# Query tiles in pairs, value products over 512 queries, and one written order for five engines in a hybrid attention block

## The chip, the cores and the metric

The kernel runs on one core of a Trainium2 chip. The metric is the time of one execution on the device, in microseconds; the time of a version is the median of its runs. A profiled execution gives a span, from the first to the last instruction, and a record of each instruction on TensorE (PE, with PEld for its weight loads), VectorE (DVE), ScalarE (ACT), GpSimd (POOL) and SyncE (SP, which issues DMAs).

## The reference

One block of a model with 512 tokens of 1024 features, all in float32. Two attention branches work on one projection of the normalised input and are merged by gates; an output projection and a feed-forward part with squared relu follow, each added to the residual.

```python
n = rmsnorm(h, g_mix[l])
proj = n @ w_in[l]
(gq, gk, gv, gr, z_gf, z_gb, cq, ckv, kr, z_ma, z_mb) = jnp.split(proj, SPLIT_IDX, axis=-1)
y_gla = gla_branch(...)
y_mla = mla_branch(cq, ckv, kr, positions, g_q[l], w_uq[l], g_kv[l], w_ukv[l])
merged = jax.nn.sigmoid(z_ma) * y_gla + jax.nn.sigmoid(z_mb) * y_mla
h = h + merged @ w_out[l]
m = rmsnorm(h, g_mlp[l])
h = h + jnp.square(jax.nn.relu(m @ w_ff1[l])) @ w_ff2[l]
...
return rmsnorm(h, g_final)
```

`gla_branch` is linear attention with 4 heads in both directions. `mla_branch` is softmax attention with 8 heads: queries of 96 features (64 and 32 that are rotated by position), keys of the same make, values of 128.

```python
def attend(qblk):
    s = jnp.einsum('bhqd,bhkd->bhqk', qblk, kt).astype(jnp.float32)
    p = jax.nn.softmax(s, axis=-1)
    return jnp.einsum('bhqk,bhkv->bhqv', p.astype(vt.dtype), vt)
```

## The kernel before, in words

**Numbers in two parts.** Almost every product is made of three matmuls in the type fp32r (`mm3`, L87 to L90): each operand is split into a high part (a copy in fp32r, on ACT) and a remainder (a subtraction, on DVE or POOL; `split`, L92 to L94), and high times high, high times remainder and remainder times high are added up in PSUM. So each line L88, L89 or L90 in the profile is one of the three, and L93 and L94 are the two halves of a split. Tiles ending in h and l, or pairs of tiles, are these parts.

**Stages.** First come the input projections, with a seven-product scheme for large blocks (`Seven`). Then a loop over the first three linear heads, and the fourth, last one behind it (L1310 on), among which the latent projections for the softmax heads, the rotary tables and the gates zb4 to zb7 are made. From L1350 the softmax attention runs, with the first products of the output projection at its end; then the rest of the output projection (`wo_product`, seven products m over two row blocks, in the PSUM tiles wox, wow and woz) and its row statistics (hp). From L1888 the feed-forward part runs, eight phases f0, g0 to f3, g3, whose steps are written with due times and sorted. `last_rows` ends it: the last product of the last phase, and the final rmsnorm.

**Softmax attention.** A head is in `heads` with its query tile q (one tile of two parts, 128 x 2 x 512, made in `up_units` from uq and the rotated rows ro, which SP copies into its rows 64 to 95), its keys kbuf, and its values. Four query tiles of 128 each go through these steps, one loop turn n a tile:

- `att_scores` (L1095): three matmuls into s, the row maximum (top, L1102, DVE), the exponential with the row sum (e, L1107, ACT).
- `att_normalise` (L1110), for two tiles: the reciprocal and two scalings, one on ACT (L1113), one on DVE (L1114).
- `att_flip` (L1116), three turns after the scores: four transposes (L1122) of e into tp, split into pT, a pair of tiles for each half of the queries.
- `att_values` (L1127), six turns after: for one half, 256 queries, and four key blocks, 12 matmuls of 256 columns into av.
- `merge` (L1143), once for both halves (for head 7 once for each): the gate times av on DVE (tb, L1150), and two additions on POOL (mx, my, L1153). After every second head `merged_sums` makes yo and zo on POOL, and these and mx are split into gao, ghyo and glyo, ghzo and glzo, the left sides of the output projection.

**What sets the order.** A scheduler orders each engine's instructions unless the code holds it. `in_program_order` ties an engine's instructions from one point on into one chain; `goes_behind` places one group behind another on some engines. PE, ACT and DVE are held to the written order up to the gate zb7 and then again from L1790 on; in between, in attention, PE, ACT and DVE are the scheduler's, apart from a dozen `goes_behind`. POOL is chained in program order from `pooled`, with another chain from `attending`. SP is chained from `stepped` on. `last_rows` has a chain of its own (L1786), which on POOL isn't tied to what stands before it: its first instructions can be placed among the last steps of the feed-forward part.

**The tail.** For each of four row blocks i there are: the sum of squares of the right half (`out_first`, L1713, ACT) and of the left (`out_square`, L1723, ACT); the mean of the first (`out_mean`, L1717, POOL); the row times the gain for the right half (`out_gained`, L1720, POOL); the factor (`out_rstd`: L1727 on DVE, the power L1730 on POOL); the left half (`out_left`, L1734, DVE), the right half (`out_right`, L1738, ACT) and the stores (L1743). The left half of block 3 is made in two parts of 256 columns, gend0 and gend1, each added by L1754; L1776 takes its mean and first part together.

Of the kernel before, what the change touches and what calls it, by code (L numbers as in the profile page):

```python
# [18 lines left out]
P = 128  # L19
# [35 lines left out]

@with_exitstack
def tile_block(ctx: ExitStack, tc: tile.TileContext, t, out: bass.AP):
    nc = tc.nc
# [76 lines left out]
    make_identity(nc, ident)  # L135
# [887 lines left out]
    def up_units(pr):  # L1023

        wq = stage(3, P, f"wq{pr}")
        for k in range(3):
            nc.sync.dma_start(
                wq[:, k, :].rearrange("p (h e) -> p h e", h=2), w_uq[:, k, 2 * pr : 2 * pr + 2, 0:NOPE]
            )
        wqh, wql = halves(3, P, f"wq{pr}")  # L1030
        split(wqh, wql, wq, nc.gpsimd)
        wk = stage(2, 384, f"wk{pr}")
        nc.sync.dma_start(
            wk.rearrange("p k (h e) -> p k h e", h=2), w_ukv[:, :, 2 * pr : 2 * pr + 2, :]
        )
        wh, wl = halves(2, 384, f"wk{pr}")
        src = wk.rearrange("p k (h e) -> p k h e", h=2)
        for k in range(2):
            for c, e in ((slice(0, 128), slice(0, NOPE)), (slice(128, 384), slice(NOPE, 192))):
                split(wh[:, k, c].rearrange("p (h e) -> p h e", h=2),  # L1040
                      wl[:, k, c].rearrange("p (h e) -> p h e", h=2), src[:, k, :, e], nc.gpsimd)
        if pr == 0:
            yield
        def rotary_rows(i):
            h = (2 * pr + i) * HALF
            for x in range(2):
                at = NOPE + x * HALF
                nc.sync.dma_start(raw(qs[i][at : at + HALF]), raw(ro[x][h : h + HALF]))

        apart = pr in (0, MH // 2 - 1)
        qs = [u4(f"q{pr}{i}") for i in range(2)]
        for i in range(2):
            if apart or i == 1:
                rotary_rows(i)
        yield
        accq = up_T(wqh, wql, cq, f"uq{pr}")
        if apart:
            for i in range(2):  # L1060
                split_scaled(qs[i][0:64, 0, :], qs[i][0:64, 1, :], accq[i * 64 : i * 64 + 64, :], QK_SCALE)
        else:
            split_scaled(qs[0][:, 0, :], qs[0][:, 1, :], accq, QK_SCALE)
# [31 lines left out]
    def att_scores(head, qt):  # L1095
        q, kb, _, _ = heads[head]
        tok = slice(qt * P, (qt + 1) * P)
        acc = ps("at", f"s{head}{qt}")
        d = slice(0, NOPE + ROPE)
        mm3(acc, q[d, 0, tok], q[d, 1, tok], kb[d, 0, :], kb[d, 1, :], True, True)  # L1100
        top = sm("top", 1)
        nc.vector.tensor_reduce(top, acc, axis=AX.X, op=ALU.max, negate=True)  # L1102
        e = u2(f"e{head}{qt}")
        if qt % 2 == 0:
            tots[head] = sm("tot", 2)
# [10 lines left out]
    def att_flip(head, qt):  # L1116
        e = probs.pop((head, qt))
        if qt % 2 == 0:
            pTs[head, qt // 2] = [u4(f"pT{head}{qt}{x}", F32R, (P, NT, 256)) for x in range(2)]
        tp = ps("at", f"tp{head}{qt}")  # L1120
        for k in range(NT):
            nc.tensor.transpose(tp[:, k * P : (k + 1) * P], e[:, k * P : (k + 1) * P], ident)  # L1122
        hi, lo = pTs[head, qt // 2]
        c = slice((qt % 2) * P, (qt % 2 + 1) * P)
        split(hi[:, :, c], lo[:, :, c], tp.rearrange("p (k q) -> p k q", k=NT))

    def att_values(head, half):  # L1127
        if half == 0:
            avs[head] = ps("mm", f"av{head}")
        acc = avs[head]  # L1130
        hi, lo = pTs.pop((head, half))
        _, _, vs, c = heads[head]
        for k in range(NT):
# [3 lines left out]
        if head < MH - 1:  # L1137
            if half == 1:
                merge(head, acc, (0, 1))
        else:  # L1140
            merge(head, acc, (half,))
# [167 lines left out]

    h = GH - 1  # L1310
# [27 lines left out]
    first_units = traced()  # L1338
# [3 lines left out]
    first_units = first_units, traced()  # L1342
    at = traced()
    zb = proj_run(w_b, xT)
    last_gate = at, traced()
    g2.append(gated(zb, "b7")[1])
    in_program_order(fixed, SPLITTERS)
    in_program_order(ordered, PE_ONLY)
    in_program_order(pooled, (mybir.EngineType.Pool,))
# [14 lines left out]
    at = traced()  # L1364
    next(units)
    goes_behind((at, traced()), first_units, SPLITTERS[:1])
    attending = traced()
    sums_of, flipping, span = {}, {}, {}
    for n in range(4 * MH + LAG_C - 1):
        if n % 2 == 0 and 2 <= n <= 4 * MH:  # L1370
            att_normalise((n - 2) // 4, (n - 2) % 4)
        scored = traced()
        if n < 4 * MH:
            att_scores(n // 4, n % 4)
            if n - 2 in flipping:
                goes_behind((scored, traced()), flipping[n - 2], SPLITTERS)
        scored = scored, traced()
        if n == 0:
            goes_behind(scored, last_gate, PE_ONLY)
        if n == 3:  # L1380
            span["fourth"] = scored
        if 2 <= n % 8 < 7:
            at = traced()
# [3 lines left out]
            if n < 4:  # L1387
                goes_behind((at, traced()), scored, PE_ONLY)
        if n in (6, 14):
            units = up_units(n // 8 + 2)  # L1390
            at = traced()
            next(units)
            if n == 6:
                goes_behind((at, traced()), span["fourth"], SPLITTERS[:1])
        b = n - LAG_B
        if n == 30:
            xs_ = wo_accs[1] = [ps("mm", f"wox{rb}") for rb in range(2)]
            at = traced()
            wo_product(1, ps_=(0,))
            begun = at, traced()  # L1400
            goes_behind(begun, scored, PE_ONLY)
        if 0 <= b < 4 * MH:
            flips = traced()
            att_flip(b // 4, b % 4)
            flipping[n] = flips, traced()
            if n == 30:
                goes_behind(flipping[n], begun, PE_ONLY)

        if n == 20:
            load_onto(B11, B12, w_out)  # L1410
        extra = traced()
# [8 lines left out]
        if n < 4 * MH:  # L1420
            goes_behind((extra, traced()), scored, SPLITTERS[:1])
# [7 lines left out]
        if n == 17:  # L1429
            at = traced()  # L1430
            load_wo(B21, B22)
            span["sums"] = at, traced()
# [6 lines left out]
        if c >= 0 and c % 2 == 1:  # L1439
            valued = traced()  # L1440
            att_values(c // 4, (c % 4) // 2)
            valued = valued, traced()
        if n == 35:
            at = traced()
            split_first(wo_left[2], merged[2][0], "o2")
            goes_behind((at, traced()), valued, SPLITTERS[1:])
# [298 lines left out]
    def last_rows(ph):  # L1745

        begun = traced()
# [10 lines left out]
        for i in (2, 3):  # L1758
            out_first(i)
        out_gained(2)  # L1760
        out_mean(2)
# [8 lines left out]
        out_mean(3)  # L1770
# [3 lines left out]
        out_store(1)  # L1774
        p = hparts[3]
        nc.vector.scalar_tensor_tensor(p[:, 2:3], p[:, 1:2], 1.0 / D, p[:, 2:3], op0=ALU.mult, op1=ALU.add)  # L1776
        last_part(1)
# [8 lines left out]
        in_program_order(begun)  # L1786

    begun = traced()  # L1790
# [8 lines left out]
    att_values(MH - 1, 1)  # L1799
# [8 lines left out]
    at = traced()  # L1808
    f0.load(B11)
    goes_behind((at, traced()), span["sums"], SP_ONLY)  # L1810
# [74 lines left out]
    for x in range(2):  # L1885
        f0.lo(2, x)
        m_lo(2, x)
    FIRST, SECOND, PERIOD = 36, 22.77, 7857  # L1888
# [75 lines left out]
    stepped = traced()  # L1964
# [34 lines left out]
```

## Time and profile before

| | us |
|---|---|
| runs | 738.37, 738.38, 739.01 |
| median | 738.38 |
| profiled execution | 739.02 |
| its span | 737.3 |
| first written instruction of the changed stretch on PE (products bd) | 254.6 |
| last matmul starts | 728.32 |

A line of a timeline gives start, duration, engine, line, operation, the tiles written and read, the shapes, and in square brackets how long the engine sat idle before it and whose work ended that. A line of the groups gives the count, the busy time, the mean duration in ns, then the idle time before them. A line of a table by stretches gives the stretch, its length, busy time of PE, PEld, DVE, ACT and POOL, each with the number of instructions, the clock that was granted to PE, the busy share of the DMA engines and GB/s. A wait gives who waited, for whom, the sum in us, how often, and the longest.

### The profile page before, as it was taken

To read this page: it belongs to the slowest core of one execution; us is meant where nothing else is said; L and a number is where in the kernel's file an instruction comes from. 1 tells how busy PE (TensorE), PEld (TensorE's weight loads), DVE (VectorE), ACT (ScalarE), POOL (GpSimd) and SP (SyncE) were. 2 spreads that over 40 slices of the span, in tenths; PEclk is the share of its full clock that TensorE was granted. 3 is DMA by queue.
4 is the path that set the end of the run, shared out by engine and by line. 5 is a ranking of instruction groups with operands and counts; after the bars stand their busy time and mean duration, and the time that the engine had idled before them with its cause. 6 is when DMAs were issued, how large, how long until landed. Compare 5 with 4: busy or idle time off the path is not lost.

```text
span 737.3 us, 11473 instructions
## 1 busy us (share of the span) xinstructions
PE 726.9 (99%) x4226; PEld 643.1 (87%) x4226; DVE 625.0 (85%) x861; ACT 494.2 (67%) x809; POOL 220.7 (30%) x284
## 2 busy tenths in 40 slices
PE   9999999999999999999999999999999999999995
PEld 7888888888888888899888899889988998899984
DVE  7777787889988788798898889998699869987896
ACT  7557465595696675988856879545874477537764
POOL 0732020243743724126852511200211012101215
PEclk9999999999999999999999999999999999999999
DMA  9849682431222324557978899862987088815773
GB/s 309 277 100 215 215 188 90 79 64 31 58 58 58 51 72 89 127 111 214 291 145 233 133 267 185 184 204 63 250 181 192 20 240 175 196 57 146 170 114 114
DMA packets 80520, 109.95 MB, mean 149 GB/s; under 512 B 15920, under 2 KB 34352, under 8 KB 80464
## 3 DMA queue, kind: packets, MB, share of 16 engines
q1 hardware_dynamic: 63088, 75.64, 32.9%
q0 software_dynamic: 17088, 33.30, 27.1%
q8 instruction: 33, 0.54, 0.3%
q10 hardware_dynamic: 288, 0.28, 0.1%
q14 instruction: 23, 0.19, 0.1%
HBM read 104.22 MB, written 2.10 MB: 144 GB/s over the span
## 4 chain that ended last, share of the span: by engine, by line
PE 88%; DVE 5%; issue 2%; POOL 2%; ACT 1%; DMA 1%; POOLq 0%; DVEq 0%; ACTq 0%
PE first L326 3%; PE tp L1122 2%; PE zb L88 1%; PE zb L89 1%; PE zb L90 1%; PE f2x L90 1%; PE f3x L90 1%; PE f1x L90 1%; PE f3x L89 1%; PE f2x L89 1%; PE f1x L89 1%; PE f1x L88 1%; PE f3x L88 1%; PE f2x L88 1%; PE av L89 1%
## 5 line engine op out<-in xcount | busy, mean ns | idle before, releaser
L1626 POOL DMA_DIRECT2D w<-in_w_ff x40 | 48.3, 1240 | 254.9 <-DMA w<-in_w_ff 139.3
L1102 DVE TENSOR_REDUCE top<-s 128x1 f32<-128x512 f32 x32 | 21.6, 682 | 4.9 <-PE s L90 4.7
L1107 ACT ACTIVATE e<-s,top 128x512 f32<-128x512 f32 x32 | 21.9, 687 | 3.5 <-DVE top L1102 2.6
L94 DVE TENSOR_TENSOR pT<-tp,pT 128x512 fp32r<-128x512 f32 x32 | 21.8, 682 | 2.4 <-ACT pT L93 2.0
L93 ACT ACTIVATE pT<-tp 128x512 fp32r<-128x512 f32 x32 | 19.0, 595 | 3.2 <-PE tp L1122 3.2
L1122 PE MATMUL tp<-ident,e 128*128 128x128 f32 x128 | 19.4, 274 | 0.0
L88 PE MATMUL av<-pT,v 128*128 128x256 f32 x64 | 19.1, 299 | 0.0
L90 PE MATMUL av<-pT,v 128*128 128x256 f32 x64 | 18.2, 285 | 0.0
L89 PE MATMUL av<-pT,v 128*128 128x256 f32 x64 | 18.1, 284 | 0.0
L1122 PEld LDWEIGHTS tp<-ident,e 128*128 128x128 f32 x128 | 15.2, 140 | 3.1 <-ACT e L1113 0.7
L94 POOL TENSOR_TENSOR qF<-qk,qF 128x512 fp32r<-128x512 f32 x4 | 6.6, 1641 | 37.6 <-ACT qF L93 37.6
L667 POOL DMA_DIRECT2D gvw<-in_w_in x4 | 4.8, 1230 | 38.7 <-DVE gvw L672 34.0
L667 POOL DMA_DIRECT2D zaw<-in_w_in x4 | 4.9, 1228 | 32.7 <-DVE zaw L672 28.0
L1628 DVE TENSOR_TENSOR w<-w,w 128x1024 f32<-128x1024 f32 x12 | 14.4, 1220 | 0.1
L980 POOL DMA_DIRECT2D w<-in_w_out x10 | 12.2, 1400 | 6.5 <-DVE bo60l L94 5.3
L88 PE MATMUL s<-kbuf,q 96*128 96x512 f32 x32 | 14.1, 439 | 0.0
L1153 POOL TENSOR_TENSOR mx<-tb,yg 128x256 f32<-128x256 f32 x8 | 7.7, 964 | 19.8 <-DVE tb L1150 13.9
L577 ACT ACTIVATE bds<-bd 128x512 f32<-128x512 f32 x4 | 2.4, 597 | 15.8 <-PE bd L555 15.8
L89 PE MATMUL s<-kbuf,q 96*128 96x512 f32 x32 | 12.6, 395 | 0.0
L90 PE MATMUL s<-kbuf,q 96*128 96x512 f32 x32 | 12.6, 393 | 0.0
L1113 ACT ACTIVATE e<-e,tot 128x512 f32<-128x512 f32 x16 | 11.6, 726 | 1.3 <-DVE tot L1112 1.3
L89 PEld LDWEIGHTS av<-pT,v 128*128 128x128 f32 x64 | 12.2, 191 | 0.2
(2156 smaller groups left out, 3250.4 us busy)
## 6 DMA issues: line engine op xcount, KB each, us to landing
w<-in_w_ff SPq DMA_DIRECT2D x48, 512.0 KB, 5.6
w<-in_w_ff POOLq DMA_DIRECT2D x40, 512.0 KB, 6.2
w<-in_w_out POOLq DMA_DIRECT2D x10, 512.0 KB, 8.3
grw<-in_w_in SPq DMA_DIRECT2D x8, 512.0 KB, 8.6
zaw<-in_w_in SPq DMA_DIRECT2D x8, 512.0 KB, 7.4
gvw<-in_w_in SPq DMA_DIRECT2D x8, 512.0 KB, 4.7
w<-in_w_out SPq DMA_DIRECT2D x16, 256.0 KB, 5.6
w220f<-in_w_ff SPq DMA_DIRECT2D x8, 512.0 KB, 6.2
```

Source lines behind the costliest of these rows:

```text
L88: nc.tensor.matmul(acc, lh, rh, start=start, stop=False, skip_group_check=onto)
L89: nc.tensor.matmul(acc, lh, rl, start=False, stop=False, skip_group_check=onto)
L90: nc.tensor.matmul(acc, ll, rh, start=False, stop=stop, skip_group_check=onto)
L93: nc.scalar.activation(hi, src, AF.Copy)
L94: rest.tensor_tensor(lo, src, raw(hi), op=ALU.subtract)
L326: nc.tensor.matmul(f_accs[i], a[:, i * P : (i + 1) * P], b, start=k == 0 and x == 0, stop=k == KD - 1 and x == 2)
L980: nc.gpsimd.dma_start(d, rows.rearrange("(k t p) w -> p t k w", t=2, p=P)[:, x // 2], accum_op=ALU.add)
L1102: nc.vector.tensor_reduce(top, acc, axis=AX.X, op=ALU.max, negate=True)
L1107: nc.scalar.activation(e, acc, AF.Exp, bias=top, accum_out=tot[:, qt % 2 : qt % 2 + 1])
L1122: nc.tensor.transpose(tp[:, k * P : (k + 1) * P], e[:, k * P : (k + 1) * P], ident)
L1626: nc.gpsimd.dma_start(d, self.source(src, g), accum_op=ALU.add)
L1628: nc.vector.tensor_tensor(d, d, self.tiles(src)[g], op=ALU.add)
```

## The change

Query tiles of attention are transposed in pairs: `att_flip` takes a head and a half, and fills for two key blocks at a time one PSUM tile with two query tiles; pT is now four tiles a head, 128 x 2 x 512, each with two key blocks and all 512 queries. `att_values` makes both halves in one go, with matmuls of 512 columns, for heads 0 to 6, and one half at a time for head 7. A query tile is two tiles, one for each part, so each copy by SP is issued twice. The maxima and sums get names of their own.

From the last linear head on, no call reaches the engines at once: a wrapper holds them by engine and tile, and then emits them in a written sequence, which covers the linear head, attention and the output projection. All engines, SP and POOL too, are chained in that order, and so are the feed-forward part and the last rows behind it. In `last_rows` the means of blocks 2 and 3 come before the gain product of block 2, and the products and the addition of gend1 come before L1776.

The diff, cut to its core; entries of the sequence are engine (P for PE, A for ACT, D for DVE, G for POOL, S for SP), tile, and a count:

```diff
+class Held:
...
+    def hold(self):
+        self.held = {}
+
+    def emit(self, sequence):
+
+        held, self.held = self.held, None
+        for entry in sequence.split():
+            name, _, count = entry.partition("*")
+            for _ in range(int(count or 1)):
+                what, args, options = held[name].pop(0)
+                what(*args, **options)
...
@@ -1045,12 +1086,13 @@
             for x in range(2):
                 at = NOPE + x * HALF
-                nc.sync.dma_start(raw(qs[i][at : at + HALF]), raw(ro[x][h : h + HALF]))
+                for y in range(2):
+                    nc.sync.dma_start(raw(qs[i][y][at : at + HALF]), raw(ro[x][h : h + HALF, y]))
...
-        qs = [u4(f"q{pr}{i}") for i in range(2)]
+        qs = [[u2(f"q{pr}{i}{y}", F32R) for y in range(2)] for i in range(2)]
...
-            nc.sync.dma_start(raw(qs[1][0:64]), raw(qs[0][64:128]))
+            split_scaled(*qs[0], accq, QK_SCALE)
+            for y in range(2):
+                nc.sync.dma_start(raw(qs[1][y][0:64]), raw(qs[0][y][64:128]))
...
-    def att_flip(head, qt):
-        e = probs.pop((head, qt))
-        if qt % 2 == 0:
-            pTs[head, qt // 2] = [u4(f"pT{head}{qt}{x}", F32R, (P, NT, 256)) for x in range(2)]
-        tp = ps("at", f"tp{head}{qt}")
-        for k in range(NT):
-            nc.tensor.transpose(tp[:, k * P : (k + 1) * P], e[:, k * P : (k + 1) * P], ident)
-        hi, lo = pTs[head, qt // 2]
-        c = slice((qt % 2) * P, (qt % 2 + 1) * P)
-        split(hi[:, :, c], lo[:, :, c], tp.rearrange("p (k q) -> p k q", k=NT))
-
-    def att_values(head, half):
+    def att_flip(head, half):
         if half == 0:
+            pTs[head] = [[u4(f"pT{head}{x}{k}") for k in range(2)] for x in range(2)]
+        es = [probs.pop((head, 2 * half + i)) for i in range(2)]
+        cols = slice(half * HT, (half + 1) * HT)
+        for g, (hi, lo) in enumerate(zip(*pTs[head])):
+            tp = ps("at", f"tp{head}{half}{g}")
+            for i, e in enumerate(es):
+                for k in range(2):
+                    at = k * HT + i * P
+                    nc.tensor.transpose(tp[:, at : at + P], e[:, (2 * g + k) * P : (2 * g + k + 1) * P], ident)
+            split(hi[:, :, cols], lo[:, :, cols], tp.rearrange("p (k q) -> p k q", k=2))
+
+    def att_values(head, halves_):
+        if head not in avs:
             avs[head] = ps("mm", f"av{head}")
...
         for k in range(NT):
             vt = vs[k // 2]
-            mm3(acc[:, half * 256 : (half + 1) * 256], vt[:, 0, k % 2, c], vt[:, 1, k % 2, c],
-                hi[:, k, :], lo[:, k, :], k == 0, k == NT - 1)
...
+            mm3(avs[head][:, cols], vt[:, 0, k % 2, c], vt[:, 1, k % 2, c],
+                his[k // 2][:, k % 2, cols], los[k // 2][:, k % 2, cols], k == 0, k == NT - 1)
+        merge(head, avs[head], halves_)
...
+    in_program_order(fixed, SPLITTERS)
+    in_program_order(ordered, PE_ONLY)
+    in_program_order(pooled, (mybir.EngineType.Pool,))
+    nc.hold()
+    written = traced()
     h = GH - 1
...
-        if c >= 0 and c % 2 == 1:
-            valued = traced()
-            att_values(c // 4, (c % 4) // 2)
-            valued = valued, traced()
+        if c >= 0 and (c % 4 == 3 or c == 4 * MH - 3):
+            att_values(c // 4, (0, 1) if c // 4 < MH - 1 else (0,))
...
         for i in (2, 3):
             out_first(i)
+        out_mean(2)
+        out_mean(3)
         out_gained(2)
-        out_mean(2)
         add_rows(2, 0, acc)
...
         out_square(3, cols[0])
-        out_mean(3)
         out_gained(3)
...
+        last_part(1)
         p = hparts[3]
         nc.vector.scalar_tensor_tensor(p[:, 2:3], p[:, 1:2], 1.0 / D, p[:, 2:3], op0=ALU.mult, op1=ALU.add)
-        last_part(1)
         out_square(3, cols[1], 0)
...
-        in_program_order(begun)
...
+    SEQUENCE = """
...
+        P:gla3o1*12 D:kbuf0 P:gla3o0*6 D:roa1 A:gla3sq P:gla3o1*6 D:zb4 A:gla3sq A:wk0h D:ro0 A:gla3sq S:wq1f
+        D:ckvhl1 S:q111 A:gla3sq D:ckvc0 A:tb4 G:gla3ss G:wk0l A:ckvhl0 G:wk0l A:zb7h G:gla3ss D:ckvhl0 G:gla3ss
+        G:wk0l D:roa1 S:wq2f S:q000 A:ro1 S:q001 S:q211 S:kbuf3 P:zb6*24 A:wq1h S:kbuf2 D:zb6 G:wq1l S:q000 D:ro1
+        S:q011 P:uk0*6 S:q010 A:kbuf0 S:w2_00 S:q111 D:kbuf0 S:q001 S:wq2f S:q110 P:uq0*9 S:wk2f A:q000 A:tb6
+        D:q001 A:q010 D:zb7l P:uq1*9 A:q100 P:y15*4 D:grb S:wk1f A:kbuf1 D:grb P:s00*3 D:top00 S:q011 P:s01*3
...
+        A:bo21h D:pT410 G:w2_00 D:q311 A:bo20h P:av3*12 A:e52 D:tb3 P:s61*3 A:pT401 D:tot52 D:top61 G:my1 P:tp500*4
+        A:pT500 P:tp501*4 D:pT411 G:yo0 P:av4 A:e61 G:yo1 D:pT510 P:av4*4 A:e52 G:w2_01 D:e53 D:v30 A:pT501 P:s60*3
+        G:mx1 D:pT511 P:s62*3 G:w2_20 D:top60 P:tp510*4 A:pT500 D:top62 A:v31 G:yo1 D:bo20l A:e60 G:w2_11 P:av4*7
+        A:e62 P:s63*3 G:zo0 D:top63 P:wox1*3 P:av5 G:zo1 D:tot60 D:pT510 A:e63 P:tp511*4 D:e61 A:pT501 D:v31
...
+        P:wox1*3 D:pT611 G:w2_10 P:tp611*4 D:tot72 A:pT601 P:tp701*4 A:ghzo0 P:tp700*4 G:glyo0 P:wox0*2 A:pT700
+        A:pT701 P:wow1*3 G:yo2 P:av6 A:ghyo1 D:pT711 G:mx2 P:wow1*3 D:pT611 G:w2_20 A:gao2 D:pT710 A:ghyo2 A:e72
+        D:glyo2 A:bo50h D:e73 P:av6*11 D:tb6 P:wow0*3 D:gao2 G:mx3 P:av7*5 D:bo50l G:zo2 P:tp710*4 A:pT700
+        P:tp711*4 A:ghzo1 D:pT710 S:w2_00 P:wox0*3 A:gao3 G:glzo1 A:pT701 P:wow0*3 D:gao3 D:bo21l S:w2_30 A:bo51h
+        P:wox1*3 G:my3 S:h0 G:w2_21 P:av7*7 D:tb7 S:h3 P:wox0*3 D:pT711 G:zo2 P:woz0*3 D:bo51l G:mx3 G:glyo1 A:gao3
...
+        P:woz1*3 D:glbo3 A:bo30h P:wow1*3 D:zo3 D:h0 P:wox1*3 A:bo61h P:wox1*3 A:ms0 D:bo61l P:wox0*3 G:hp0
+        G:glzo0 P:woz0*3 D:h1 P:woz1*3 D:h2 G:w2_21 P:woz1*3 A:bo31h D:h3 P:wox1*3 D:gdo0 D:bo30l P:wox0*3 A:ghco3
...
+    """
+    nc.emit(SEQUENCE)
...
-    in_program_order(begun, PE_ONLY + SPLITTERS)
-    in_program_order(stepped, SP_ONLY)
-    in_program_order(attending, (mybir.EngineType.Pool,))
     last_rows(g3)
+    in_program_order(written)
```

In the changed program POOL's last instructions stand in this order: mean 0, gain product 0, mean 1, gain product 1, powers 0 and 1, means 2 and 3, gain product 2, power 2, gain product 3, power 3. Before they were: mean 0, gain product 0, mean 1, gain products 1 and 2, mean 2, powers 0, 1 and 2, mean 3, gain product 3, power 3.

More of the change, by code (lines that the diff above doesn't have):

```diff
@@ L53, in shape_constants, with __init__, __getattr__, called @@
     return c
+class Held:
+    ENGINES = {"tensor": "P", "scalar": "A", "vector": "D", "gpsimd": "G", "sync": "S"}
+    def __init__(self, nc):
+        self.nc, self.held = nc, None
+    def __getattr__(self, name):
+        x = getattr(self.nc, name)
+        return HeldEngine(self, self.ENGINES[name], x) if name in self.ENGINES else x
+    def hold(self):
[7 more added lines that the diff above has]
+                what(*args, **options)
+        assert not any(held.values()), {k for k, x in held.items() if x}
+class HeldEngine:
+    def __init__(self, holder, letter, engine):
+        self.holder, self.letter, self.engine = holder, letter, engine
+    def __getattr__(self, op):
+        what = getattr(self.engine, op)
+        def called(*args, **options):
+            held = self.holder.held
+            if held is None:
+                return what(*args, **options)
+            tile_name = args[0].tensor.name.rsplit("_", 2)[0]
+            held.setdefault(self.letter + ":" + tile_name, []).append((what, args, options))
+        return called
 @with_exitstack
 def tile_block(ctx: ExitStack, tc: tile.TileContext, t, out: bass.AP):
-    nc = tc.nc
+    nc = Held(tc.nc)
     sb = ctx.enter_context(tc.tile_pool(name="sb", bufs=1))
@@ L1099, in att_scores @@
         d = slice(0, NOPE + ROPE)
-        mm3(acc, q[d, 0, tok], q[d, 1, tok], kb[d, 0, :], kb[d, 1, :], True, True)
-        top = sm("top", 1)
+        mm3(acc, q[0][d, tok], q[1][d, tok], kb[d, 0, :], kb[d, 1, :], True, True)
+        top = sm(f"top{head}{qt}", 1)
         nc.vector.tensor_reduce(top, acc, axis=AX.X, op=ALU.max, negate=True)
@@ L1104, in att_scores @@
         if qt % 2 == 0:
-            tots[head] = sm("tot", 2)
+            tots[head] = sm(f"tot{head}{qt}", 2)
         tot = tots[head]
@@ L1363, in tile_block @@
     units = up_units(1)
-    at = traced()
     next(units)
-    goes_behind((at, traced()), first_units, SPLITTERS[:1])
-    attending = traced()
-    sums_of, flipping, span = {}, {}, {}
+    sums_of = {}
     for n in range(4 * MH + LAG_C - 1):
```

105 lines of the change are left out of this document (51 added, 54 removed).

## The prediction

> **What bounds the kernel now.** I read the page's first two parts, then TensorE's starts one by one, then the stretch the change rewrites, then the last 12 us.
>
> ```profile
> span 737.3 us, 11473 instructions
> PE 726.9 (99%) x4226; PEld 643.1 (87%) x4226; DVE 625.0 (85%) x861; ACT 494.2 (67%) x809; POOL 220.7 (30%) x284
> PE   9999999999999999999999999999999999999995
> PEclk9999999999999999999999999999999999999999
> ```
>
> TensorE (PE) is busy in every slice but the last, at full clock, so only fewer or shorter matmuls, or fewer gaps between them, can shorten the body; behind its last matmul stands a tail. Busy time overlaps (a matmul's duration is longer than its distance to the next), so I price by starts, from the timeline:
>
> ```profile
> 339.58 0.29 PE L89 MATMUL av<-pT,v 128*128 128x256 f32 x1
> ...
> 340.77 0.28 PE L90 MATMUL av<-pT,v 128*128 128x256 f32 x1
> ...
> 335.13 0.40 PE L88 MATMUL uq<-cqhl,wq3h 128*128 128x512 f32 x1
> ...
> 336.27 0.39 PE L90 MATMUL uq<-cqhl,wq3l 128*128 128x512 f32 x1
> ```
>
> Here av are the value products, uq a 512-wide projection. Ten steps of av take 1.19 us, 0.119 each; five of uq take 1.14, 0.228 each. Gaps are rare. The waits of PE from 254 us (where the rewritten stretch begins) to 425:
>
> ```profile
> PEld tp L1122 <- ACT e L1113: 0.7, 3, 0.3
> PEld wox L89 <- DVE bo40l L94: 0.5, 1, 0.5
> PEld f0w L89 <- DVE ml L1512: 0.3, 1, 0.3
> PEld wox L90 <- DVE gao L94: 0.3, 1, 0.3
> ```
>
> Together 1.8 us: all that a better order could give back in 170 us. But around 370 to 410 us, where attention ends and the output projection starts, VectorE (DVE) is as full as PE:
>
> ```profile
> 370.00:380.00 10.00, 10.00 (x59) 8.54 (x58) 9.86 (x12) 5.72 (x9) 6.77 (x7) 1.00 0.58 92
> 380.00:390.00 10.00, 10.00 (x46) 8.29 (x45) 9.68 (x15) 6.21 (x11) 3.52 (x4) 1.00 1.02 234
> 390.00:400.00 10.00, 10.00 (x46) 8.29 (x45) 9.12 (x15) 5.17 (x11) 1.50 (x3) 1.00 1.09 281
> 400.00:410.00 10.00, 9.91 (x52) 8.04 (x51) 8.49 (x13) 9.44 (x19) 4.70 (x5) 1.00 0.67 150
> ```
>
> The third, fifth and seventh numbers are PE, DVE and POOL. DVE idles 0.14 + 0.32 + 0.88 + 1.51 = 2.85 us in 40.
>
> **The change, part by part.** Counted in both programs' instruction lists: PE 4172 becomes 4088, DVE 863, ACT 748 and POOL 289 stay, SP 219 becomes 237.
>
> *Values 512 wide.* Heads 0 to 6 had 7 x 24 products of 256 columns and get 7 x 12 = 84 of 512; head 7 keeps its 24. Each pair cost 0.238 and becomes 0.228: 84 x 0.010 = 0.87 us less with unrounded steps, all of it on PE, which nothing covers. Bounds 0 and 1.3 (a step read 0.003 off).
> [...]
>
> *Transposes in pairs of query tiles.* 128 before and after. Whether four or eight stand together makes no difference:
>
> ```profile
> 299.68 0.44 PE tp L1122 x4
> ...
> 210.86 0.87 PE y L791 x8
> ```
>
> 0.11 us each, both ways: nothing. The splits behind them keep their count and 128x512 size. A flip now needs both tiles of its pair normalised; the written order puts other products between, so I take nothing, with the wait's present 0.7 us either way as bounds.
>
> *Query tiles as two.* Every rotary copy is issued once for each half:
>
> ```profile
> L1048 SPq DMA_DIRECT2D q<-ro x16: 507/544/591, 282.6 to 327.5; - x16
> DMA to landing us min/median/max: 2.2/2.4/3.5
> L371 DVE TENSOR_TENSOR zb<-zb,R 128x512 f32<-128x512 f32 x4 | 2.6, 678 | 0.0
> ```
>
> 18 more issues of 0.54 are 9.8 us of SP, whose own time no engine sees; what counts is the first score. In the written order the last of its four copies (q001 from ro1) stands behind another (q111), both behind DVE's ro1, that behind DVE's zb6, which waits for the last zb6 product. From there PE has 24 products of 0.228 and four transposes: 5.5 + 0.44 = 5.9 us. The copies need 0.68 + 0.68, two issues (1.1) and a landing of 2.4 to 3.5: 4.9 to 6.0. I take 0; 1.2 if the landing is slow and an issue more is in the way.
>
> *One written sequence.* Beside the copies no instruction is added; the order on all five queues from the last linear head to the first feed-forward phase is replaced (behind it PE's, DVE's and ACT's orders are the old ones up to the last rows). Its best is the whole 1.8 us, its worst a new wait. Early loads of the output weights move ahead on SP, bo20l leaves the full stretch on DVE (now it comes before the scores of head 6 are done), which relieves DVE by
>
> ```profile
> L94 DVE TENSOR_TENSOR bo20l<-bo20f,bo20h 128x1024 fp32r<-128x1024 f32 x1 | 1.2, 1211 | 0.0
> ```
>
> On the other side four remainders on POOL, which before were done by 364 us, the two glyo and two glzo, now stand among the merges of heads 4 to 7, that is in the full stretch:
>
> ```profile
> L94 POOL TENSOR_TENSOR glyo<-yo,ghyo 128x512 fp32r<-128x512 f32 x2 | 2.6, 1290 | 0.3 <-ACT ghyo L93 0.3
> ...
> 345.57 1.70 POOL L94 TENSOR_TENSOR glzo<-zo,ghzo 128x512 fp32r<-128x512 f32 x1
> ...
> 362.52 1.29 POOL L94 TENSOR_TENSOR glzo<-zo,ghzo 128x512 fp32r<-128x512 f32 x1 [2.73 <-ACT ghzo L93]
> ...
> 340.90 0.48 DVE L1114 TENSOR_SCALAR e<-e,tot 128x512 f32<-128x512 f32 x1
> ...
> 346.38 1.18 DVE L1114 TENSOR_SCALAR e<-e,tot 128x512 f32<-128x512 f32 x1
> ```
>
> The same DVE operation takes 0.48 alone and 1.18 beside POOL's glzo: one stood still for the other. Four of 1.29 are 5.2 us. Against them stand the 2.85 us of idle and 1.2 of bo20l, and DVE's additions from PSUM, which the tail below shows undisturbed beside POOL (0.42 at 729.96, beside 1.26). So I let it cost nothing and give back half of the 1.8 us: -0.9, bounds -1.8 and +2.7 (worked out under the rivals).
> [...]
>
> *Factor steps reordered.* The tail:
>
> ```profile
> 725.11 1.29 POOL L1720 TENSOR_TENSOR ms<-h,gfin 128x512 f32<-128x512 f32 x1
> 726.35 0.67 DVE L1465 TENSOR_TENSOR h<-h,ge 128x512 f32<-128x512 f32 x1
> 726.40 0.19 ACT L1713 ACTIVATION_READ_ACCUMULATOR ms<-h 128x1 f32 x1
> 726.75 1.08 POOL L1730 TENSOR_TENSOR hp<-hp,mhalf 128x1 f32<-128x1 f32 x2
> 727.35 0.75 DVE L1734 SCALAR_TENSOR_TENSOR ms<-h,hp,gfin 128x512 f32<-128x512 f32 x1 [0.33 <-POOL hp L1730]
> 728.32 0.28 PE L90 MATMUL gend<-g341h,f3l 128*128 128x256 f32 x1
> 728.58 0.99 POOL L1730 TENSOR_TENSOR hp<-hp,mhalf 128x1 f32<-128x1 f32 x1 [0.74 <-DVE hp L1727]
> 729.88 0.16 DVE L1776 SCALAR_TENSOR_TENSOR hp<-hp 128x1 f32<-128x1 f32 x1 [0.71 <-POOL hp L1717]
> 729.93 1.26 POOL L1720 TENSOR_TENSOR ms<-h,gfin 128x512 f32<-128x512 f32 x1
> 729.96 0.42 DVE L1754 TENSOR_TENSOR h<-gend,h 128x256 f32<-128x256 f32 x1
> 730.29 1.45 DVE L1734 SCALAR_TENSOR_TENSOR ms<-h,hp,gfin 128x512 f32<-128x512 f32 x1
> 732.47 0.75 DVE L1734 SCALAR_TENSOR_TENSOR ms<-h,hp,gfin 128x512 f32<-128x512 f32 x1 [0.66 <-POOL hp L1730]
> ```
>
> DVE's wait of 0.71 for a factor of row block 3 goes, as its mean is taken earlier: that is the gain, at most 0.7. But the new order holds on POOL too: the powers of blocks 0 and 1, the means of 2 and 3, and only then the gain product of block 2, which before ran at 725.11. Mean 3 waits for ACT's sum (726.59), so that product starts near 726.9, just as DVE's L1734 of block 0 becomes ready at 727.0. If POOL is first, L1734 ends near 728.2 + 0.5 = 728.7 instead of 728.10 (at 730.29 it ended 0.55 after POOL's operation); the addition, L1734 of block 1 and the last addition follow at 729.1, 729.8 and 730.1 (before 730.38: that part gains). POOL's power of block 2 waits for block 1's L1734 as now (0.99) and ends at 730.2, its gain product of block 3 (1.26) and DVE's L1734 of block 2 share until 732.1, then 0.2, 0.55 and 0.75 with their handovers: 733.5 against 733.22, 0.3 later. If DVE is first it comes out 0.1 later. I take +0.2; bounds -0.7 and +0.4.
>
> **Sum**, for the profiled execution (739.02 us; its span 737.3 and 1.7 around it): -0.87 - 0.9 + 0.2 = -1.6, 737.4. It was the slowest of the three; their median is 738.38, so 736.8.
>
> **Rivals.**
> *Everything comes back:* the four waits go, and the tail stays even: 738.38 - 0.87 - 1.8 = 735.7. For it: the waits are short and of different kinds. Against: every order has some.
> [...]
> *DVE and POOL take turns in the full stretch* (the other side): of the 5.2 us, 4.1 are added after bo20l, and 1.2 remain if all idle time takes its part; between them 2.7. PE waits as long at the output products: 738.38 - 0.87 + 0.2 + 2.7 = 740.4. It makes the change slower from 0.7 us on, measurably from 2.2. For it: the 1.18 row, and a DVE idle for 0.14 us in ten. Against: DVE's queue there also holds PSUM additions, beside which POOL can work.
> *The query copies come late:* +1.2 on the forecast, 738.0.
>
> **How the numbers follow.** Measurable means 0.2%, 1.48 us: below 736.90 or above 739.86. Forecast 0.45 (own range 736.2 to 737.4; 0.27 of it below 736.90), everything back 0.15, places changed 0.13, turns 0.22, late copies 0.05. Faster 0.27 + 0.15 = 0.42, same 0.18 + 0.13 + 0.05 = 0.36, slower 0.22. The range runs from 735.4 (everything back and 0.3 from the tail) to 740.4.
>
> **What would show it.** 84 av matmuls of 512 columns 0.228 us apart; PE's first feed-forward product 1 to 2.5 us earlier; PE waits under 1 us in that stretch. Wrong: PE waits on bo or gl tiles with DVE operations of 128x1024 well over 1.22 us (turns); a first score waiting on a copy of q; a tail, from the last matmul's end (728.6) to the end of the span 8.7 us now, that is shorter by over 0.5 or longer by as much.

## The result, and the profile after

The changed kernel takes 750.88 us (median of 4 runs, 749.74 to 751.72) against 738.57 (4 runs): a ratio of 1.0165, 95% interval 1.0147 to 1.0183. It is slower by 12.3 us, where 1.6 less was forecast, and it lies 10.5 us beyond the upper end of the range. The profiled execution, whose span is 748.0 us, took 749.74, the least of the four: the last 1.1 us up to the median stand in no trace.

The first lines of its page:

```profile
span 748.0 us, 11320 instructions
PE 727.8 (97%) x4142; PEld 639.2 (85%) x4142; DVE 625.3 (84%) x861; ACT 496.1 (66%) x809; POOL 223.9 (30%) x284
PE   9999999999999998999999999999999999999995
```

PE's busy time has hardly moved (726.9 before), but the span is 10.7 us longer, so PE now waits; one slice has an 8. The PE instructions behind attention are the same in both kernels, so their starts show where the time went. The last product ckv, ahead of the rewritten stretch, starts at 249.23 us (248.92 before), the first feed-forward product f0x at 423.45 (412.50), the last matmul at 738.89 (728.32). So 0.31 was there before the stretch, 10.64 are lost in it, 0.38 are won at the start of the feed-forward part (the old wait at 421 us is gone), and the tail, 9.0 us before, is 9.1. The waits of PE in that stretch, who waited, for whom, sum, count, longest:

```profile
PE s L76 <- DMA q<-ro: 2.7, 1, 2.7
PE tp L76 <- DVE tot L76: 1.4, 1, 1.4
PE av L76 <- DVE tb L76: 1.1, 1, 1.1
PE s L76 <- DMA kbuf<-kbuf: 1.0, 1, 1.0
PE sc L76 <- ACT bds L76: 0.8, 1, 0.8
PE gla3st L76 <- DVE kT L76: 0.8, 1, 0.8
PE woz L76 <- POOL glyo L76: 0.6, 1, 0.6
PE wox L76 <- DVE bo60l L76: 0.6, 1, 0.6
PE tp L76 <- DVE pT L76: 0.3, 1, 0.3
PE uv L76 <- POOL wk3l L76: 0.2, 1, 0.2
```

Before, the same view, asked for PE, lists no wait at all here: the four of the prediction's list, 1.8 us in all, are waits of PEld, whose loads run beside PE's matmuls (643.1 us of loads and 726.9 of matmuls in the span of 737.3). By the distances between PE's starts less a step (gaps of over 0.15 us), PE lost 0.25 us before in this stretch and loses 11.8 now. The four old waits are gone, and ten others stand in their place. The largest is about a quarter of the loss, and they have several causes:

| at us | lost | what was late |
|---|---|---|
| 288.3 to 289.0 | 3.2 | first score: a copy of q |
| 309.4 | 1.2 | first score of head 2: a copy of kbuf |
| 342.4 | 1.6 | transposes: e, behind pT on DVE, behind DMAs |
| 386.6, 391.9, 396.4 | 1.2 + 0.8 + 1.1 | tb and bo60l on DVE, glyo on POOL |
| 257.8, 265.8 | 0.9 + 1.0 | bds on ACT, kT on DVE |
| 348.9, 374.4 | 0.4 + 0.4 | wk3l on POOL, pT on DVE |

**SP's queue.** The SP entries of the timeline before the first score, start and length of each group:

```profile
282.95 0.37 SPq L76 DMA_DIRECT2D wq2f<-in_w_uq  x1
283.36 1.82 SPq L76 DMA_DIRECT2D q<-ro  x3
285.29 1.17 SPq L76 DMA_DIRECT2D kbuf<-kbuf  x2
286.56 1.81 SPq L76 DMA_DIRECT2D q<-ro  x3
288.47 0.53 SPq L76 DMA_DIRECT2D w<-in_w_out  x1
289.09 1.14 SPq L76 DMA_DIRECT2D q<-ro  x2
```

SP never rests here. The last of the four copies that the first score needs is the second of the last group, 289.65 to 290.23; DVE's ro1, from which it copies, had ended at 283.99. Between them SP issued eight other DMAs at 0.6 us each, and the score needed only one of those. The score went on at 292.09. At 342 us it is the same queue in another place:

```profile
338.54 0.44 SPq L76 DMA_DIRECT2D h<-in_x  x1
339.09 1.14 SPq L76 DMA_DIRECT2D q<-ro  x2
...
341.38 0.51 SPq L76 DMA_DIRECT2D q<-ro  x1
...
343.36 0.69 DVE L76 TENSOR_TENSOR pT<-tp,pT 128x512 fp32r<-128x512 f32 x1 [1.93 <-DMA w<-in_w_out]
```

DVE stood 1.93 us at a split that waits for six DMA queues. The view names a load, but that load went on landing until 344.3. The last landing that was complete on these queues when the split started is that of the copy out of the rotated rows ro issued at 339.09: it took 4.0 us (2.3 is the median of such copies) and ended at 343.09. On SP it stood behind two loads, of w and h, which the run on SP's order below moves behind it. The last copy out of ro, issued at 341.38, landed at 345.2, behind the split's start, so the split did not wait for it.

**DVE and POOL.** The two engines at 382 to 389 us, DVE's large splits first, then POOL:

```profile
382.75 1.77 DVE L76 TENSOR_TENSOR bo50l<-w,bo50h 128x1024 fp32r<-128x1024 f32 x1
...
385.37 2.31 DVE L76 TENSOR_TENSOR bo21l<-bo21f,bo21h 128x1024 fp32r<-128x1024 f32 x1
...
388.54 1.60 DVE L76 TENSOR_TENSOR bo51l<-w,bo51h 128x1024 fp32r<-128x1024 f32 x1
```

```profile
383.40 1.73 POOL L76 TENSOR_TENSOR zo<-mx,my 128x256 f32<-128x256 f32 x1
385.08 1.52 POOL L76 TENSOR_TENSOR glzo<-zo,ghzo 128x512 fp32r<-128x512 f32 x1
386.56 1.70 POOL L76 TENSOR_TENSOR my<-tb,yg 128x256 f32<-128x256 f32 x1
```

Two of these splits before:

```profile
377.94 1.21 DVE L94 TENSOR_TENSOR bo21l<-bo21f,bo21h 128x1024 fp32r<-128x1024 f32 x1
379.07 1.75 DVE L94 TENSOR_TENSOR bo50l<-w,bo50h 128x1024 fp32r<-128x1024 f32 x1
```

Before, bo21l took 1.21, bo51l 1.22 and bo50l 1.75, as it stood beside an addition on POOL already. Here they take 2.31, 1.60 and 1.77, 1.5 us more together, and POOL's additions, 0.73 with nothing beside them, take 1.7. This is the rival of turns, in the place that it named.

### The profile page after: what moved, and what is told of

Its sections match the earlier page's. It is cut to its first block, busy times and chain, and to the rows that moved or that the text cites. A ratio compares the mean times of both kernels' runs of the same rounds, so it can differ in the third digit from the quotient of the medians.

```text
span 748.0 us, 11320 instructions
## 1 busy us (share of the span) xinstructions
PE 727.8 (97%) x4142; PEld 639.2 (85%) x4142; DVE 625.3 (84%) x861; ACT 496.1 (66%) x809; POOL 223.9 (30%) x284
## 4 chain that ended last, share of the span: by engine, by line
PE 87%; DVE 4%; POOL 3%; DMA 2%; issue 1%; ACT 1%; SPq 0%; POOLq 0%; DVEq 0%; ACTq 0%
PE first L90 3%; PE f3x L90 3%; PE f2x L90 3%; PE f1x L90 3%; PE f0x L90 3%; PE g2x L90 3%; PE g1x L90 3%; PE g0x L90 3%; PE gvx L90 3%; PE zax L90 3%; PE grx L90 3%; PE av L76 2%; PE wox L76 2%; PE s L76 2%; PE gk L90 2%; PE cq L90 2%
## 5 line engine op out<-in xcount | busy, mean ns | idle before, releaser
L90 POOL DMA_DIRECT2D w<-in_w_ff x34 | 41.0, 1205 | 249.4 <-DMA w<-in_w_ff 138.5
L76 DVE TENSOR_REDUCE top<-s 128x1 f32<-128x512 f32 x32 | 21.6, 683 | 10.7 <-PE s L76 10.7
L76 PE MATMUL s<-kbuf,q 96*128 96x512 f32 x96 | 26.3, 398 | 3.9 <-DMA q<-ro 2.7
L76 PE MATMUL av<-pT,v 128*128 128x512 f32 (+1 forms) x108 | 25.3, 373 | 1.1 <-DVE tb L76 1.1
L76 PEld LDWEIGHTS s<-kbuf,q 96*128 96x128 f32 x96 | 17.4, 189 | 7.8 <-issue 3.5
L76 PEld LDWEIGHTS av<-pT,v 128*128 128x128 f32 x108 | 18.6, 188 | 4.7 <-DVE tb L76 1.5
L76 PE MATMUL tp<-ident,e 128*128 128x128 f32 x128 | 16.8, 273 | 1.7 <-DVE tot L76 1.4
L76 POOL DMA_DIRECT2D w<-in_w_out x10 | 15.2, 1536 | 6.5 <-DVE bo60l L76 4.5
L76 POOL TENSOR_TENSOR mx<-tb,yg 128x256 f32<-128x256 f32 x8 | 7.3, 916 | 10.6 <-DVE tb L76 10.6
L90 ACT ACTIVATE f2h<-f2a 128x512 fp32r<-128x512 f32 x10 | 6.1, 621 | 6.2 <-DVE f2a L90 6.2
L90 ACT ACTIVATE f3h<-f3a 128x512 fp32r<-128x512 f32 x10 | 6.1, 620 | 6.2 <-DVE f3a L90 6.2
L90 ACT ACTIVATE f0h<-f0a 128x512 fp32r<-128x512 f32 x10 | 6.1, 620 | 6.2 <-DVE f0a L90 6.2
```

Source lines behind the costliest of these rows:

```text
L76: what(*args, **options)
L90: return what(*args, **options)
```

## The experiments

**Pairs and wide values alone,** in the kernel before: `att_flip`, `att_values` and the turns at which they are called from the change, query tiles whole, order as before.

```diff
-            att_flip(b // 4, b % 4)
-            flipping[n] = flips, traced()
+            if b % 2:
+                att_flip(b // 4, b % 4 // 2)
+                flipping[n] = flips, traced()
...
-        if c >= 0 and c % 2 == 1:
+        if c >= 0 and (c % 4 == 3 or c == 4 * MH - 3):
...
```

> The kernel before with the transposes in pairs and the values 512 wide; query tiles whole, engines ordered as before. If the loss comes from the written sequence (from SP's queue or from DVE and POOL taking turns), this shows the wide values alone: 738.6 - 0.9 = 737.7. If pairs hurt by themselves, because a flip waits for two normalised tiles, PE waits on tot or e and the time is 740 or more.

741.68 us against 738.49 of the kernel before: 1.0040 (1.0025 to 1.0055). PE's timeline at the first value product:

```profile
306.63 0.40 PE L90 MATMUL s<-kbuf,q 96*128 96x512 f32 x1
308.58 0.50 PE L88 MATMUL av<-pT,v 128*128 128x512 f32 x1 [1.55 <-ACT pT L93]
308.92 0.42 PE L88 MATMUL uq<-cqhl,wq2h 128*128 128x512 f32 x1
...
309.99 0.63 PE L89 MATMUL av<-pT,v 128*128 128x512 f32 x1
310.41 0.63 PE L90 MATMUL av<-pT,v 128*128 128x512 f32 x1
```

Head 0's first product needs all four query tiles now, and waits 1.55 us for the last split. It is not the wait on tot or e that was named. And behind it the steps are 0.43 us instead of 0.23. The granted clock, the last but two of the numbers, in the 3.4 us that hold the wait and in the next 3.4:

```profile
305.74:309.15 3.41, 1.60 (x7) 0.97 (x7) 2.60 (x5) 3.41 (x11) 2.89 (x5) 1.00 0.73 171
309.15:312.56 3.41, 3.41 (x10) 2.65 (x9) 2.48 (x5) 2.09 (x4) 0.00 (x0) 0.50 0.45 120
```

No sum had a term for this: eight steps, 1.6 us more.

**Head 0 in halves.** The same kernel, but head 0's value products in two halves of 256 columns, with one merge.

```diff
+        if c in (1, 3):
+            att_values(0, (c // 2,), c == 3)
-        if c >= 0 and (c % 4 == 3 or c == 4 * MH - 3):
+        elif c >= 0 and (c % 4 == 3 or c == 4 * MH - 3):
...
```

> The kernel of pairs in the old order, with head 0's value products in two halves of 256 columns. If its loss is the first 512-wide product waiting for the last split of head 0 (1.6 us) and the half clock behind it (9 steps 0.2 us longer): 741.7 - 3.4 + 0.1 = 738.4. If pairs delay every head alike: 741 to 742.

738.92 against 738.68: 1.0002 (0.9993 to 1.0011); of the 3.2 us, 0.2 are left (-0.5 to 0.8). So the loss of the kernel above was that one wait and the clock behind it.

**The wait filled.** The kernel of pairs again, with matmuls of no use in the place of the wait.

```diff
+            if c == 3:
+                avs[0] = ps("mm", "av0")
+                at = traced()
+                for _ in range(7):
+                    nc.tensor.matmul(avs[0][:, 0:P], ident, ident, start=True, stop=True)
+                goes_behind((at, traced()), scored_at[7], PE_ONLY)
...
```

> The kernel of pairs in the old order, with seven matmuls of the identity (no use of their result) on PE in the place where it waited 1.7 us for the last split of head 0; three of the query products also come ahead of the first value product. If the half clock behind that wait (8 steps of 0.2 us) came from PE's idle time, it goes: 741.7 - 1.6 - 0.5 (real work put into the wait) = 739.6, though PE has more to do. If idle time has nothing to do with the clock: 741.2, and the half clock is there again.

740.66 against 738.63: 1.0026 (1.0017 to 1.0036), 1.0 less than without the filling, though PE has 14 matmuls more in the records. But the two intervals overlap, and 740.66 lies between the two times expected, so the times decide nothing. The trace says more. PE's filling, and the clock around it and behind it:

```profile
306.65 1.73 PE L1445 MATMUL av<-ident 128*128 128x128 f32 x14
```

```profile
305.06:308.47 3.41, 3.16 (x25) 2.77 (x24) 2.60 (x6) 3.41 (x11) 3.01 (x5) 1.00 0.60 130
308.47:311.88 3.41, 3.41 (x20) 2.87 (x19) 3.15 (x6) 2.61 (x6) 0.29 (x1) 1.00 0.56 160
```

PE is idle for 0.25 us instead of 1.81, and the clock stays whole. This is one profiled execution of each kernel; what other traces show of the half clock stands in the last section.

**Split query tiles alone,** in the kernel before.

```diff
-                nc.sync.dma_start(raw(qs[i][at : at + HALF]), raw(ro[x][h : h + HALF]))
+                for y in range(2):
+                    nc.sync.dma_start(raw(qs[i][y][at : at + HALF]), raw(ro[x][h : h + HALF, y]))
...
```

> The kernel before with each query tile as two tiles, so 18 more issues by SP, and nothing else. Theory of the copies, strong form (the issues cost wherever they stand): 2 to 6 us more, 740.6 to 744.6. Weak form (they cost only where the written order queues them ahead of what a score needs): 738.6, within 0.7. Theory of turns: 738.6.

743.45: 1.0063 (1.0047 to 1.0080). The size fits the strong form; the trace doesn't. DVE and PE at the first score:

```profile
293.51 0.69 DVE L1104 TENSOR_REDUCE top<-s 128x1 f32<-128x512 f32 x1 [3.96 <-PE s L90]
294.22 0.69 DVE L94 TENSOR_TENSOR kbuf<-uk,kbuf 64x512 fp32r<-64x512 f32 x1
294.92 0.88 DVE L782 SCALAR_TENSOR_TENSOR grb<-gla3o,gla3ss,grb 128x256 f32<-128x256 f32 x2
```

```profile
293.08 0.39 PE L90 MATMUL s<-kbuf,q 96*128 96x512 f32 x1
295.86 0.50 PE L88 MATMUL s<-kbuf,q 96*128 96x512 f32 x1 [2.38 <-DVE grb L782]
```

The scheduler had put the first row maximum on DVE ahead of kbuf, grb and grc. DVE stood 3.96 us at it, and the second score waited for the PSUM tile that grb reads. (The half clock followed here too: 0.51 from 297.4 to 300.8.)

**The maximum tied behind.** The same kernel and one line.

```diff
             goes_behind(scored, last_gate, PE_ONLY)
+            goes_behind(scored, first_units, SPLITTERS[1:])
```

> The kernel of the split query tiles again, with one tie more: on DVE the first row maximum stays behind the gating of the last linear head, where it is in the kernel before. If the 5 us of that kernel came from this maximum alone, which stood ahead of the additions that free the PSUM tile of the second score: 738.6, within 0.7, with the same 18 issues. If they came from the issues: 741 or more.

739.25 against 738.68: 1.0008 (0.9999 to 1.0017). So the loss came from this maximum, as the trace said. The 18 issues themselves cost 0.6 us (-0.1 to 1.3, not clear of nothing), where little that is needed stands behind them.

**SP's order.** Now in the changed kernel: SP's entries moved at three places of the sequence.

```diff
-S:q211 S:kbuf3 ... S:kbuf2 ... S:q000 D:ro1 S:q011 ... S:q010 ... S:w2_00 S:q111 ... S:q001
+S:q000 D:ro1 S:q001 S:q211 S:kbuf3 S:kbuf2 S:q011 ... S:q010 ... S:w2_00 S:q111
...
-S:bo11f S:w2_01 ... S:q101 ... S:q100 ... S:kbuf2
+S:q101 ... S:q100 ... S:kbuf2 S:bo11f S:w2_01
...
-S:w2_31 S:h2 ... S:q310 ... S:q310 ... S:w2_30 S:w2_00 ... S:q300
+S:q310 ... S:q310 ... S:q300 S:w2_00 S:w2_30 S:h2 S:w2_31
```

> The changed kernel with SP's entries alone moved at three places: the copies that the first score, the first score of head 2 and the last use of the rotated rows wait for go ahead of copies and loads that nobody waits for yet. Theory of the copies: the three PE waits (3.2, 1.2 and 1.6 us) go, 745 to 747 against 750.9. Theory of turns: 750 to 751, as DVE and POOL keep their order. If every wait only moves: 749 to 750.

747.01: 3.9 us less than the changed kernel, at the upper end of what was expected of the copies. PE's waits from 280 to 350 us:

```profile
PE s L76 <- ACT e L76: 1.6, 2, 1.4
PE y L76 <- DVE q L76: 0.5, 1, 0.5
```

The three waits of 6.0 us are gone, and others of 2.9 (by starts) have come. By PE's starts SP's queue is the largest part of the loss, 6.0 of 11.8, and about half of what is won there comes back at the next late instruction. The times alone do not rank it ahead of the next part (2.9): runs of one kernel lie 2 to 3 us apart here.

**Four remainders left out.** The changed kernel without POOL's glyo and glzo of the first two head pairs.

```diff
+        if name in ("yo0", "zo0", "yo1", "zo1"):
+            nc.scalar.activation(h, src, AF.Copy)
+            l = h
```

> The changed kernel without POOL's four remainders glyo and glzo of the first two head pairs (left out: the high part stands in for them; all matmuls stay). Theory of turns: POOL leaves DVE 5.8 us between 376 and 402, the PE waits on tb, glyo and bo60l (3.1 us) shrink to under 1.5, 748 to 749.4 against 750.9. Theory of the copies: 750.9, within 0.7.

748.03: 2.9 less. From 370 to 410 us PE waits once:

```profile
PE tp L76 <- DVE pT L76: 0.3, 1, 0.3
```

All 3.1 us are gone. But this kernel takes two things away at once, operations that DVE takes turns with and the remainder that woz waited for, and bo50l, bo21l and bo51l still take 1.75 each (5.3 together, 4.2 before): what the written order leaves on POOL beside them is mostly additions, and only bo21l gains (it had 2.31). The traces tell a part apart. From the start of bo50l to that of bo60l DVE needs 11.6 us instead of 14.0: 1.6 of the 2.4 are shorter operations of its own, which I put down to turns, and 0.7 is a wait for ACT, which had waited for POOL. And woz's wait (0.8 by starts) was for POOL's remainder itself, so POOL was simply late there.

**The start, and all three.** bds and kT on ACT ahead of wr1h and cqhl, with SP's order; then with the remainders left out as well.

```diff
-A:cos A:wr1h A:cqhl0 G:wr1l P:bd*4 S:wq0f P:kt*4 S:wr0f A:kT A:wk0h A:bds
+A:cos P:bd*4 A:bds S:wq0f P:kt*4 A:kT A:wr1h G:wr1l A:cqhl0 S:wr0f A:wk0h
```

> The changed kernel with SP's entries in the order of the run on SP's order, and bds and kT on ACT ahead of wr1h and cqhl; nothing left out. If the two waits of PE at the start of the sequence (0.9 and 1.0 us) come from ACT standing at wr1h, whose weights land late: 747.0 - 1.9 = 745.1. If from DVE's own work: 747.0.

> The changed kernel with three things at once: SP's entries in the order of the run on SP's order, POOL's four remainders left out (the high part stands in for them) and, at the start of the sequence, bds and kT on ACT ahead of wr1h and cqhl. If the causes add up: 750.9 - 3.9 - 2.9 - 1.9 = 742.2. If waits only change places: 744 or more.

747.42 and 743.60. The first missed: the start gives nothing (747.0 without it). PE's wait for bds goes, but that for kT grows from 0.96 to 1.36, and in the profiled execution a score then waits 2.3 us for ACT; the granted clock over the whole span is 0.992 there, 0.995 in the changed kernel. The second lies 1.4 above the sum of the causes; its waits:

```profile
PE s L76 <- ACT e L76: 2.8, 2, 1.5
PE gla3st L76 <- DVE kT L76: 1.2, 1, 1.2
PE s L76 <- DVE pT L76: 0.9, 1, 0.9
PE y L76 <- DVE q L76: 0.5, 1, 0.5
PE tp L76 <- DVE pT L76: 0.3, 1, 0.3
```

What is left, 4.9 us over the kernel before, are waits on ACT and DVE: for kT and for one pT where the changed kernel waits too, the others at new places.

**The change without its sequence,** then with the two ties that the runs above had found.

> The whole change but its written sequence: pairs, wide values, split query tiles and the new last rows, with the engines ordered as in the kernel before. If the two misplacements seen so far both come (first maximum on DVE 5.0, first wide product 3.2): 738.7 + 5.0 + 3.2 + 0.2 = 747; then the written sequence is worth 4 us of the loss. If the order comes out without one of them: 742 to 744.

> The same with the first maximum tied behind the gating on DVE and head 0's values in halves. If these two places are all that the change costs outside its sequence: 738.9 (the run of head 0 in halves) + 0.6 (18 issues) + 0.2 (last rows) = 739.7; the written sequence then stands for 11 us. If copies or pairs cost elsewhere: 741 or more.

747.32 (1.0118, 1.0101 to 1.0134) and 743.34 (1.0059, 1.0044 to 1.0074). The first agrees with the sum of the two misplacements (747), and its trace has both waits (for the second the view names a copy of q, but ACT's pT ended 0.05 us ahead of the product). The second isn't 739.7: at 350 us one score waits 1.54 us for ACT's e, where the kernel with head 0 in halves waits 0.2; matmuls of 512 columns behind it stand 0.42 us apart, and the granted clock is 0.73 from 351.0 to 354.4. Pairs and split tiles together give the scheduler another order than either alone. So the change loses 8.7 us without its sequence, and 4.8 with the two ties: its sequence adds 3.6 or 7.5 us to that, and is not the whole loss.

**Scores behind the wide products.**

> The kernel with head 0 in halves, and on PE each wide value product ahead of the next score, so that PE has work where it stood 0.8 us in three waits of scores on ACT. If the waits go: 738.9 - 0.6 = 738.3, under the kernel before. If ACT and DVE then stand without scores and the waits come back at the transposes: 739 to 740.

738.80 against 738.58. The tie left every engine's order as it was, so this is the kernel with head 0 in halves measured a second time. No version was faster than the kernel before.

## Why the prediction was wrong, point by point

Two steps failed. The sum for the copies of q left out the queue that they stand in: 0, at most 1.2, was put, and SP's queue cost 3.2 us at the first score and 6.0 at three places. And the upper bound of the written sequence, +2.7, priced one new wait, where ten came, 11.8 us together with those for the copies.

- *Values 512 wide, -0.87.* Right as the size of a step: by the medians a wide step is 0.227 us and a narrow one before 0.120, so 84 x 0.013 = 1.1, within the bounds. No run shows it as time: the kernel with head 0 in halves has 72 of the 84 and takes as long as the kernel before, as PE's starts lose 0.8 us at three new waits of scores.
- *Transposes in pairs, nothing.* The transposes cost nothing (a step of 0.109 us by the medians, before and after). In the changed kernel the term held too: there no wide product waits for a split, and the flip's one large wait (1.6 us at 342 us) came through SP's copies. But "so I take nothing, with the wait's present 0.7 us either way as bounds" was right by luck of the order: it looked at the flip and not at what the flip feeds. A wide product needs four tiles, and in the old order that alone put 1.6 us of waiting, and 3.41 us of half clock (0.50), at head 0.
- *Query tiles as two, 0, at most 1.2.* The step "the copies need 0.68 + 0.68, two issues (1.1) and a landing" counted the copies that the score waits for, and not the queue that they stand in: eight issues lay between the end of ro1 and the last copy, and SP worked through them one by one. From the end of the zb6 products to the score's going on it took 9.4 us, where 4.9 to 6.0 were added up. It cost 3.2 us there, 1.2 and 1.6 at two places that the prediction didn't price. "SP, whose own time no engine sees" was the wrong sentence: a queue that is written down is on the path of whatever stands last in it.
- *One written sequence, -0.9, bounds -1.8 and +2.7.* All four old waits went, as named, but they were not worth 1.8 us. They are waits of PEld, read as if they were PE's; by PE's starts they cost 0.25 us in the stretch and 0.38 at 421 us, so 0.6 was all there was to win, and -0.9 was out of reach. The upper bound failed by more. It priced one new wait, at the fullest place, and took the other places to be as they were. But the order of every queue was new over 170 us, and ten waits came.
- *Factor steps, +0.2.* Right in each step. The gain product of block 2 meets DVE's operation of block 0, and POOL's last power comes late:

```profile
737.49 1.84 DVE L90 SCALAR_TENSOR_TENSOR ms<-h,hp,gfin 128x512 f32<-128x512 f32 x1
...
743.31 0.75 DVE L90 SCALAR_TENSOR_TENSOR ms<-h,hp,gfin 128x512 f32<-128x512 f32 x1 [0.66 <-POOL hp L90]
```

```profile
737.48 1.29 POOL L90 TENSOR_TENSOR ms<-h,gfin 128x512 f32<-128x512 f32 x1
```

Less the 10.57 us by which all is later, the first ends at 728.76 (728.7 forecast) and the last at 733.49 (733.5 forecast). Over all profiles, the tail from the last matmul's start is 9.1 us with the new last rows (9.08 to 9.16) and 8.9 on average with the old (8.75 to 9.03).
- *The rivals.* At the place named for turns (2.7) came waits of 3.1, some of them turns and some POOL being late; late copies (1.2) came with 3.2 and more, and waits changed places. (In the sum for turns, 5.2 less 1.2 is 4.0, not 4.1; it changes little.) Of the turns there the four remainders, which it priced, made 1.6 us; POOL's additions, which it didn't, make about as much (three splits of 1.75 instead of 1.21). The rivals were given as alternatives, with chances that add to one, but nothing in them excluded each other: all three happened. Added up on the case of waits that change places (738.38 - 0.87 + 0.2 = 737.7) they would have given 741.6 and not 740.4; the rest is their size and places that were not priced.

What stays open: the 4.9 us of the three-causes kernel were not taken apart, nor the 4.8 us that the change loses without its sequence and with both ties; and PE's 3.1 us at 386 to 398 us are only in part separated into turns and POOL being late.

## What to carry to other kernels

When an order is replaced over a long stretch of a kernel whose bounding engine has no gaps, price it queue by queue: for each instruction that the bound engine waits for, count every entry ahead of it on its queue, SP's too, and ask the same of the next one behind it. Waits at different places added up here (11.8 us by starts at ten places, and PE's starts behind them 10.6 us later), so rivals of that kind belong together into the upper end of the range. A tile that gathers more before it is used makes its first use later (here by 1.7 us); let the first use be small.

## What the runs showed of the hardware

The traces of the kernel before and of the changed kernel hold two records of the granted clock each, a whole one (1.0) and behind it a half one (0.5): it changes once, in the tail, 213 and 215 times 3.41 us behind the start of the first record. That start is at 6.81 and at 7.34 us. Steps of 3.41 us in which PE was idle (length less PE's busy time) were followed by whole or by half clock. In the kernel of pairs 1.81 us of idle time were followed by half (0.50), with matmuls of 512 columns 0.43 us apart; with the wait filled 0.25 us were followed by whole (1.00). The wait of the kernel of pairs, 1.7 us by starts, lies inside one step (its two lines stand above). The changed kernel's own wait of 2.9 us is cut in two by the end of a step, 1.42 and 1.44 us idle, and the clock stays whole:

```profile
287.24:290.65 3.41, 1.99 (x10) 1.17 (x8) 2.08 (x4) 1.79 (x3) 0.00 (x0) 1.00 0.52 134
290.65:294.07 3.42, 1.98 (x9) 1.66 (x10) 1.45 (x3) 0.00 (x0) 0.00 (x0) 1.00 0.54 123
294.07:297.48 3.41, 3.41 (x17) 2.80 (x16) 2.02 (x4) 1.03 (x4) 0.46 (x1) 1.00 0.73 230
```

So the wait of 1.7 us had eight steps with 1.6 us more behind it, and the longer one had none. The idle time of a step alone does not tell the cases apart: beside the 1.81 us of the kernel of pairs, behind the last matmul of the kernel before a step with 1.84 us idle was followed by a whole one, behind that of the changed kernel one with 2.04 us by a half one. The lines, the kernel before first:

```profile
727.03:730.44 3.41, 1.57 (x14) 1.36 (x12) 2.38 (x7) 2.46 (x6) 2.50 (x5) 1.00 0.44 160
730.44:733.85 3.41, 0.00 (x0) 0.00 (x0) 2.12 (x3) 1.84 (x4) 1.30 (x2) 1.00 0.76 286
```

```profile
737.80:741.21 3.41, 1.37 (x12) 1.17 (x10) 3.37 (x7) 2.65 (x8) 2.38 (x3) 1.00 0.29 109
741.21:744.62 3.41, 0.00 (x0) 0.00 (x0) 2.19 (x3) 1.45 (x4) 1.37 (x2) 0.50 0.88 329
```

Whether the same kernel pays for a wait in one run and not in another is not shown: no kernel here has two traces.
